# Two unused tiles that shift the weight buffers by 32 bytes, in a two-layer hybrid decoder trunk

## The chip, the core and the metric

The kernel runs on one core of a Trainium2 chip, in one launch. The time is the device time of that core in microseconds (us). Five engines work side by side and meet through semaphores: TensorE (PE, with its weight loads shown apart as PEld), VectorE (DVE), ScalarE (ACT), GpSimd (POOL) and SyncE (SP, which issues most DMAs here). Lower is better.

A matmul has two operands in on-chip memory (SBUF). The stationary one, 128 columns of fp32, is put into the array by an LDWEIGHTS instruction; the moving one, up to 512 columns, is then streamed through by the MATMUL. The LDWEIGHTS of the next matmul runs while the present one streams, so that two reads of SBUF by TensorE go on at the same time, at addresses that the allocation of tiles decides.

## The reference

Two layers, each a pair of token mixers in parallel and then a gated feed-forward network, on 1024 tokens of 1024 features, all in fp32. Cut to what matters:

```python
for l in range(DEPTH):                                   # DEPTH = 2
    h = rmsnorm(x, norm1[l])
    proj = h @ w_in[l]                                   # 1024 x 5120: q, k, v of two mixers, and gates
    qa, ka, va, qb, kb, vb, gate_pre = jnp.split(proj, splits, axis=-1)
    o_a = dilated_mixture(hd4(qa, DSW_HEADS), hd4(ka, DSW_HEADS), hd4(va, DSW_HEADS))
    o_b = stick_breaking_attention(hd4(qb, SB_HEADS), hd4(kb, SB_HEADS), hd4(vb, SB_HEADS))
    g_a, g_b = split(jax.nn.sigmoid(gate_pre + b_gate[l]))
    merged = g_a * (o_a @ w_br[l, :OUT_A]) + g_b * (o_b @ w_br[l, OUT_A:])
    x = x + merged @ w_o[l]                              # 1024 x 1024
    h2 = rmsnorm(x, norm2[l])
    a, v = split(h2 @ w_up[l])                           # 1024 x 5632
    a = causal_depthwise_conv(a, conv_w[l], conv_b[l])
    x = x + (jax.nn.gelu(a, approximate=False) * v) @ w_down[l]   # 2816 x 1024
return rmsnorm(x, norm_f)
```

## The kernel before

**Arithmetic.** Each fp32 operand of a product is held in two parts of type fp32r, a rounded high part and the rest (`split`: ACT writes the high part, L145, DVE the low one, L153). A product is then three matmuls, high by high, high by low and low by high. In `seven` (L1055, its matmuls L1058 to L1060) and `product_of` (L1818 to L1820) these three stand next to each other. The large projections are done in blocks with seven products for eight (`seven` is one such product). Nearly all matmuls have 128 rows, 128 stationary columns and 512 moving columns.

**Where the operands lie.** A weight block arrives by DMA as raw fp32, and `piece` (L1049) or `weights` splits it into two tiles of 128 x 512, with the tags `wh` (high, named `w_hi`) and `wl` (low, `w_lo`), four buffers each. These eight buffers of 2048 bytes per partition are what the change moves. They serve as the stationary operand in the input projection (outputs `i_a`, `i_b`, `i_c`), the up projection (`u_a`, `u_b`, `u_c`, and `u_ps` for its first columns), the output projection (`o_ps`), and in about half of the down projection (`d_ps`; the other half has its parts in tiles `wd` of the tag `p4`). Only in two short places are they the moving operand: `v_ps<-w_hi,hh` at the very start (192 matmuls of 256 columns) and `f_ps` at the very end (36 of 512). The moving operands are activations: `hh` and `hl` (the normed input in two parts), `t_hi` and `t_lo` (sums of blocks of it) and `gd_in` (the gated values, back from DRAM).

**The order.** TensorE's order is written out by hand; ACT, DVE and POOL are scheduled, in part in written order too. In each layer there is a first stretch in which the input projection is interleaved with the attention work (transposes `sb_t` and `v_t`, scores `z`, values `sb_o`), then the output projection, the up projection and the down projection. The pool `sb` gives every tag its place in SBUF in the order in which tags are first asked for, each rounded up to 32 bytes. The tags `wh` and `wl` are first asked for in `first()`, by the first call of `weights_hi`.

Of the kernel before, what the change touches and what calls it, by code (L numbers as in the profile page):

```python
# [7 lines left out]
F32 = mybir.dt.float32  # L8
# [8 lines left out]
P = 128  # L17
# [48 lines left out]
def trunk_kernel(ctx, tc, x, norm1, vecs, w_in, w_br, w_o, w_up, w_down, norm_f, out, depth=None, probe=None):  # L66
# [6 lines left out]
    sb = ctx.enter_context(tc.tile_pool(name="sb", bufs=1))  # L73
# [300 lines left out]
    def attend(dense, items):  # L374

        late = None
        for i, (name, first, rest, rate, make) in enumerate(items):
            if i == 0:  # L380
                dense.until(first)
                dense.step()
                dense.step()
                sc, micro = make()
                for f in sc:
                    f()
                    dense.advance(rate)
                dense.done.add(name + "s")
# [269 lines left out]
    def values_on(o, todo, part_, first, last):  # L658

        todo = sorted(todo, key=lambda x: x[1].start - x[1].stop)  # L660
        for i, (vals, to, at) in enumerate(todo):
            pe.matmul(o[:, to], vals, part_[0][:, at], start=(first and i == 0), stop=False, skip_group_check=True)
        for i, (vals, to, at) in reversed(list(enumerate(todo))):
            pe.matmul(o[0:LOW, to], vals[:, 0:LOW], part_[1][:, at], start=False, stop=(last and i == 0), skip_group_check=True)
# [1345 lines left out]
    def first():  # L2010
# [17 lines left out]
        def weights_hi(r):  # L2028
            hi = sb.tile([P, 2, 256], F32R, tag="wh", bufs=4, name="w_hi")
            lo = sb.tile([P, 2, 256], F32R, tag="wl", bufs=4, name="w_lo")  # L2030
            act.copy(hi, raw[:, r : r + 2, :])
            wv.extend((hi[:, i, :], lo[:, i, :]) for i in range(2))
            parts[r] = hi, lo
# [13 lines left out]
        def scaled(i):  # L2047
            if i in (0, 2):
                rest["pair"] = big("xsq")
            sq = rest[i] = rest["pair"][:, i % 2, :] if i < 4 else sb.tile([P, T], F32, tag="ot", name="xsq")  # L2050
            ss = factor[i] = sb.tile([P, 8], F32, tag="ss", bufs=2, name="ss")
            with tc.high_priority(offset=AHEAD):
                one = act.activation(sq, xr[i], AF.Square, accum_out=ss[:, 0:1])
                if i >= TWICE + 2:
                    tc.add_manual_dep(one.ins, LAST["kept" if i == 5 else f"hi{max(2, i - 3)}"], NO_SYNC, reason="behind")
                act.activation(ss[:, 1:2], ss[:, 0:1], AF.Sqrt, bias=eps[:, 0:1], scale=1.0 / D)
                one = dve.reciprocal(ss[:, 2:3], ss[:, 1:2])
            if i == 0:
                tc.add_manual_dep(one.ins, LAST["base"], NO_SYNC, reason="in turn")
            yield  # L2060
            if i < TWICE:
                for h in range(2):
                    hd = slice(h * HF, (h + 1) * HF)
                    dve.scalar_tensor_tensor(sq[:, hd], xr[i][:, hd], ss[:, 2:3], gb[h], ALU.mult, ALU.mult)
            yield
# [48 lines left out]
        def fill(n):  # L2114

            for _ in range(n):
                pe.matmul(wp[:, 0:P], ident, ident, start=True, stop=True)
# [15 lines left out]
            pe.transpose(gb[k // 4][:, (k % 4) * P : (k % 4 + 1) * P], g0[:, k : k + 1].to_broadcast([P, P]), ident)  # L2133
        f = [scaled(i) for i in range(8)]
        next(f[0])
        weights_hi(0)
        weights_hi(2)
        fill(4)
        next(f[0])
# [90 lines left out]
```

## Time and profile before

| | |
|---|---|
| median of 3 runs | 2599.28 us (2599.11 to 2599.80) |
| profiled execution | 2600.39 us |
| its span, first to last instruction | 2598.4 us |
| PE busy in the span | 2585.0 us (99%), 12600 matmuls |
| PEld / DVE / ACT / POOL busy | 2161.4 / 2088.0 / 1340.1 / 105.5 us |
| mean granted TensorE clock | 0.999 |
| bytes moved by DMA | 470.59 MB, 181 GB/s in the mean |

A row of the groups' view gives line, engine, operation, output and inputs, shape and count, then busy time and mean duration. The duration of a MATMUL reaches from its start to its modelled end and overlaps with the next ones (some 389 ns for 512 columns); what a matmul costs in a dense stretch is the distance from its start to the next start, and that is read from the timeline, whose first column is the start in us. A row of the timeline with x4 stands for four instructions in a row.

### The profile page before, as it was taken

The page shows a single profiled execution, that of the slowest core. Times are in us where ns is not written, and L with a number is a line of the kernel's source. Part 1 is how long each engine was busy: PE and PEld are TensorE (multiplying, and loading weights), DVE is VectorE, ACT ScalarE, POOL GpSimd, SP SyncE. Part 2 cuts the span into 40 slices and gives each one's busy share as a digit, 9 for nine tenths or more (in the row PEclk, how much of TensorE's full clock was granted, in tenths as well). Part 3 has the DMA queues.
Part 4 walks back from the last instruction along what each step waited for, and adds up shares of the span by engine and source line. Part 5 has one row for each costly group of instructions (what it writes and reads, how often), then busy time and mean ns, then how long its engine had stood idle before and what let it go on. Part 6 is the DMA issues. An engine that isn't in the chain of part 4 may idle for free.

```text
span 2598.4 us, 35940 instructions
## 1 busy us (share of the span) xinstructions
PE 2585.0 (99%) x12600; PEld 2161.4 (83%) x12600; DVE 2088.0 (80%) x3482; ACT 1340.1 (52%) x2506; POOL 105.5 (4%) x145
## 2 busy tenths in 40 slices
PE   9999999999999999999999999999999999999999
PEld 8888888888888888888888888888888888888887
DVE  8878777795988888897678788777869888889966
ACT  6555666573554555422445565666645555544223
POOL 3000000030000000000000000000300000000000
PEclk9999999999999999999999999999999999999999
DMA  7534588973344444688444446798633344456963
GB/s 256 153 119 134 161 209 225 236 237 97 90 146 157 143 163 146 235 327 315 152 143 148 126 132 175 199 238 239 205 99 121 125 154 154 140 176 246 346 242 134
DMA packets 400772, 470.59 MB, mean 181 GB/s; under 512 B 24616, under 2 KB 315856, under 8 KB 398800
## 3 DMA queue, kind: packets, MB, share of 16 engines
q1 hardware_dynamic: 399728, 465.90, 56.1%
q0 software_dynamic: 704, 2.13, 0.4%
q8 instruction: 100, 1.64, 0.3%
q14 instruction: 80, 0.66, 0.1%
q10 hardware_dynamic: 160, 0.27, 0.0%
HBM read 305.59 MB, written 162.63 MB: 180 GB/s over the span
## 4 chain that ended last, share of the span: by engine, by line
PE 92%; DVE 4%; ACT 2%; DMA 1%; issue 1%; POOL 0%; DVEq 0%; ACTq 0%; POOLq 0%
PE u_a L1058 5%; PE u_a L1059 5%; PE u_a L1060 5%; PE d_ps L1818 5%; PE d_ps L1819 5%; PE d_ps L1820 5%; PE i_a L1058 5%; PE i_a L1059 5%; PE i_a L1060 5%; PE u_c L1058 3%; PE u_c L1059 3%; PE u_c L1060 3%; PE i_c L1058 2%; PE i_c L1060 2%; PE i_c L1059 2%; PE o_ps L188 2%
## 5 line engine op out<-in xcount | busy, mean ns | idle before, releaser
L145 ACT CAST w_hi<-up_a 128x512 fp32r<-128x512 f32 x280 | 173.9, 622 | 277.2 <-DVE up_a L1672 120.8
L153 DVE TENSOR_TENSOR w_lo<-up_a,w_hi 128x512 fp32r<-128x512 f32 x280 | 189.5, 689 | 83.5 <-ACT w_hi L145 83.5
L145 ACT CAST w_hi<-in_a 128x512 fp32r<-128x512 f32 x252 | 156.3, 622 | 161.6 <-PE i_c L1059 33.2
L153 DVE TENSOR_TENSOR w_lo<-in_a,w_hi 128x512 fp32r<-128x512 f32 x252 | 172.8, 688 | 72.6 <-ACT w_hi L145 60.6
L1829 DVE TENSOR_TENSOR x<-x,d_ps 128x512 f32<-128x512 f32 x220 | 150.2, 684 | 60.5 <-PE d_ps L1820 57.2
L1058 PE MATMUL u_a<-hh,w_hi 128*128 128x512 f32 x320 | 124.5, 389 | 0.0
L1060 PE MATMUL u_a<-hh,w_lo 128*128 128x512 f32 x320 | 124.5, 389 | 0.0
L1059 PE MATMUL u_a<-t_lo,w_hi 128*128 128x512 f32 x320 | 124.5, 389 | 0.0
L1060 PE MATMUL u_a<-t_hi,w_lo 128*128 128x512 f32 x320 | 124.5, 389 | 0.0
L1059 PE MATMUL u_a<-hl,w_hi 128*128 128x512 f32 x320 | 124.5, 389 | 0.0
L1058 PE MATMUL u_a<-t_hi,w_hi 128*128 128x512 f32 x320 | 124.5, 389 | 0.0
L1818 PE MATMUL d_ps<-gd_in,w_hi 128*128 128x512 f32 x316 | 123.2, 390 | 0.0
L1819 PE MATMUL d_ps<-gd_in,w_hi 128*128 128x512 f32 x316 | 123.0, 389 | 0.0
L1820 PE MATMUL d_ps<-gd_in,w_lo 128*128 128x512 f32 x316 | 123.0, 389 | 0.0
L1058 PE MATMUL i_a<-hh,w_hi 128*128 128x512 f32 x288 | 117.8, 409 | 0.0
L1058 PE MATMUL i_a<-t_hi,w_hi 128*128 128x512 f32 x288 | 116.5, 404 | 0.0
L1060 PE MATMUL i_a<-hh,w_lo 128*128 128x512 f32 x288 | 113.1, 393 | 0.0
L1060 PE MATMUL i_a<-t_hi,w_lo 128*128 128x512 f32 x288 | 113.0, 392 | 0.0
L1059 PE MATMUL i_a<-t_lo,w_hi 128*128 128x512 f32 x288 | 113.0, 392 | 0.0
L1059 PE MATMUL i_a<-hl,w_hi 128*128 128x512 f32 x288 | 112.9, 392 | 0.0
L1818 PE MATMUL d_ps<-gd_in,wd 128*128 128x512 f32 x284 | 110.9, 390 | 0.0
L1820 PE MATMUL d_ps<-gd_in,wd 128*128 128x512 f32 x284 | 110.5, 389 | 0.0
(403 smaller groups left out, 7723.4 us busy)
## 6 DMA issues: line engine op xcount, KB each, us to landing
gd<-g SPq DMA_DIRECT2D x154, 512.0 KB, 3.1
gd_in<-gd SPq DMA_DIRECT2D x154, 512.0 KB, 6.0
up_a<-in_w_up_dram SPq DMA_DIRECT2D x80, 512.0 KB, 5.4
in_a<-in_w_in_dram SPq DMA_DIRECT2D x72, 512.0 KB, 5.4
wd_raw<-in_w_down_dram SPq DMA_DIRECT2D x22, 1024.0 KB, 10.9
gin<-gs SPq DMA_DIRECT2D x32, 512.0 KB, 4.5
w_raw<-in_w_o_dram SPq DMA_DIRECT2D x64, 256.0 KB, 3.0
gs<-u SPq DMA_DIRECT2D x48, 256.0 KB, 3.2
```

Source lines behind the costliest of these rows:

```text
L145: one = act.copy(hi, src)
L153: two = dve.tensor_tensor(lo, src, f32(hi), ALU.subtract)
L188: pe.matmul(o, lh, rl, start=False, stop=False, skip_group_check=share)
L1058: pe.matmul(o, w[0][:, c], rh, start=(first and i == 0), stop=False, skip_group_check=True)
L1059: pe.matmul(o, w[0][:, c], rl, start=False, stop=False, skip_group_check=True)
L1060: pe.matmul(o, w[1][:, c], rh, start=False, stop=(last and i == 3), skip_group_check=True)
L1818: pe.matmul(o, wh[:, c], gh, start=(i == 0 and k in (0, 4, 5)), stop=False, skip_group_check=True)
L1819: pe.matmul(o, wh[:, c], gl, start=False, stop=False, skip_group_check=True)
L1820: pe.matmul(o, wl[:, c], gh, start=False, stop=(i == m - 1), skip_group_check=True)
L1829: dve.tensor_tensor(x, x, o, ALU.add)
```

## The change

In `first()`, a tile of 8 fp32 (32 bytes per partition) is asked for just ahead of the first `weights_hi`, and one of 24 fp32 (96 bytes) just behind it. Nothing writes or reads them. Since a tag gets its place when it is first asked for, the eight buffers of `wh` and `wl` stand between the two.

```diff
         f = [scaled(i) for i in range(8)]
         next(f[0])
+        sb.tile([P, 8], F32, tag="below", name="below")
         weights_hi(0)
+        sb.tile([P, 24], F32, tag="above", name="above")
         weights_hi(2)
```

`weights_hi`, which asks for the two tags, is

```python
        def weights_hi(r):
            hi = sb.tile([P, 2, 256], F32R, tag="wh", bufs=4, name="w_hi")
            lo = sb.tile([P, 2, 256], F32R, tag="wl", bufs=4, name="w_lo")
            act.copy(hi, raw[:, r : r + 2, :])
```

Start addresses in each partition, as the two programs are built:

| buffers | before | changed | before, over a multiple of 256 | changed |
|---|---|---|---|---|
| `t_hi`, `t_lo`, some `gd_in` (first of six) | 8480 | 8480 | 32 | 32 |
| `wd`, `beta` (first of four) | 57632 | 57632 | 32 | 32 |
| `w_hi` (first of four) | 86304 | 86336 | 32 | 64 |
| `w_lo` (first of four) | 94496 | 94528 | 32 | 64 |
| `hh` of the first half, some `gd_in` | 102688 | 102816 | 32 | 160 |
| `kv`, `slots` (first of four) | 151840 | 151968 | 32 | 160 |
| `hh` of the second half | 192800 | 192928 | 32 | 160 |

Before, all operands of the fp32r matmuls begin 32 bytes over a multiple of 256, and so do all the slices of them that matmuls use, since these are cut at whole 128 columns (512 bytes). After the change the weight parts alone begin at a multiple of 64 (64 over a multiple of 128), and all others still begin 32 over a multiple of 128. The instructions of each engine, and the order in which they stand, are the same in both programs.

## The prediction

> **What bounds the kernel now.** I read the page first, its busy times, its slices and its chain of waits.
>
> ```profile
> span 2598.4 us, 35940 instructions
> PE 2585.0 (99%) x12600; PEld 2161.4 (83%) x12600; DVE 2088.0 (80%) x3482; ACT 1340.1 (52%) x2506; POOL 105.5 (4%) x145
> PEclk9999999999999999999999999999999999999999
> PE 92%; DVE 4%; ACT 2%; DMA 1%; issue 1%; POOL 0%; DVEq 0%; ACTq 0%; POOLq 0%
> ```
>
> PE is busy in 99% of the span at a clock that stays at its top digit, and 92% of the chain that ended last lies on it. The view of waits, for PE alone, says how much of the rest the other engines hold:
>
> ```profile
> PE warm L2117 <- POOL ident masks.py:199: 1.8, 1, 1.8
> PE v_ps L189 <- DVE hl L153: 1.0, 2, 0.8
> PE o_ps L188 <- POOL hl L1436: 0.7, 1, 0.7
> ```
>
> The longest wait of PE on another engine is 1.8 us in all. So the time is the sum of the distances between the starts of matmuls, and a change of operand addresses can act only through them. The timeline of PE in the up projection, first and last row of 61 matmuls:
>
> ```profile
> 900.13 0.39 PE L1058 MATMUL u_a<-hh,w_hi 128*128 128x512 f32 x1
> ...
> 913.73 0.39 PE L1058 MATMUL u_a<-t_hi,w_hi 128*128 128x512 f32 x1
> ```
>
> 60 distances in 13.60 us are 226.67 ns each. The second reading is where the value projection of the second layer begins, with 256 moving columns (19 distances from the second row to the last):
>
> ```profile
> 1304.10 0.28 PE L187 MATMUL v_ps<-v_w,hh 128*128 128x256 f32 x1
> 1304.21 0.28 PE L188 MATMUL v_ps<-v_w,hh 128*128 128x256 f32 x1
> ...
> 1306.49 0.28 PE L189 MATMUL v_ps<-v_w,hl 128*128 128x256 f32 x1
> ```
>
> 2.28 us / 19 are 120.0 ns. Two points give a line: (226.67 - 120.0) / 256 = 0.4167 ns per moving column, and 226.67 - 512 x 0.4167 = 13.3 ns per matmul that do not depend on the columns streamed. The first distance here, 0.11 us, is shorter than the later 0.12: the fixed part is not simply paid at each start. These 13.3 ns are what is in question. They could be a fixed price of changing the stationary operand, or reads of the next weights that get in the way of the stream; only the second could hang on addresses.
>
> **The change part by part.** It removes and adds no instruction, moves none, and changes no wait, so nothing has a duration of its own. What changes is where eight buffers stand. How many matmuls does that touch? The counts, from the views of lines 1058 and 1059 and from the groups (durations there are minimum/median/maximum in ns; each row stands for one of the three lines of its product, and the other two have as many):
>
> ```profile
> L1058 PE MATMUL u_a<-hh,w_hi x320: 389/389/390, 711.2 to 2376.7; 128*128 128x512 f32 x160
> L1058 PE MATMUL i_a<-hh,w_hi x288: 387/395/481, 65.0 to 1817.7; 128*128 128x512 f32 x144
> L1059 PE MATMUL i_a<-hl,w_hi x288: 387/393/398, 65.2 to 1817.9; 128*128 128x512 f32 x144
> L1058 PE MATMUL u_c<-t_hi,w_hi x160: 389/389/390, 714.0 to 2363.1; 128*128 128x512 f32 x160
> L1058 PE MATMUL u_b<-hh,w_hi x160: 388/389/390, 725.4 to 2374.0; 128*128 128x512 f32 x160
> L1058 PE MATMUL i_c<-t_hi,w_hi x144: 387/394/481, 67.7 to 1798.4; 128*128 128x512 f32 x144
> L1058 PE MATMUL i_b<-hh,w_hi 128*128 128x512 f32 x144 | 59.2, 411 | 0.0
> L1818 PE MATMUL d_ps<-gd_in,w_hi 128*128 128x512 f32 x316 | 123.2, 390 | 0.0
> L187 PE MATMUL o_ps<-hh,w_hi 128*128 128x512 f32 x256 | 100.1, 391 | 0.2 <-DVE x L1327 0.2
> L187 PE MATMUL u_ps<-hh,w_hi 128*128 128x512 f32 x128 | 50.2, 392 | 0.0
> ```
>
> `u_a` and `u_c` come with both kinds of moving operand, `hh` and `t_hi`, so that they count six times: 6 x 320 + 6 x 160 + 3 x 160 = 3360 for the up projection; in the same way 6 x 288 + 6 x 144 + 3 x 144 = 3024 for the input projection; 3 x (316 + 256 + 128) = 2100 for the other three. That makes 8484 matmuls whose weights begin 32 bytes elsewhere relative to what streams beside them. One nanosecond on each would be 8.5 us, 0.33% of the time.
>
> *First term, the spacing of those 8484.* The trace has no fp32r matmul with the new distance, so it is bounded from both sides. The lower bound is the whole 13.3 ns gone: -113 us. The upper one is the worst that the same matmuls show today. That is found in the input projection:
>
> ```profile
> 302.64 0.48 PE L1058 MATMUL i_b<-hh,w_hi 128*128 128x512 f32 x1
> 302.95 0.40 PE L1059 MATMUL i_b<-hl,w_hi 128*128 128x512 f32 x1
> ...
> 304.11 0.60 PE L1294 MATMUL v_t<-ident,u 128*128 128x128 f32 x4
> 304.47 0.48 PE L1058 MATMUL i_b<-hh,w_hi 128*128 128x512 f32 x1
> 304.78 0.39 PE L1059 MATMUL i_b<-hl,w_hi 128*128 128x512 f32 x1
> ...
> 305.94 0.40 PE L662 MATMUL sb_o<-sbh,kv 128*128 128x256 f32 x2
> ...
> 306.64 0.39 PE L1059 MATMUL i_a<-hl,w_hi 128*128 128x512 f32 x1
> ...
> 307.55 0.39 PE L1060 MATMUL i_a<-hh,w_lo 128*128 128x512 f32 x1
> ```
>
> Behind a group of transposes, five matmuls take 1.16 us, 232 ns each, twice over; the four distances from 306.64 to 307.55 take 0.91 us and are back at 227. All relative addresses are the same, so the distance hangs on timing, by 5.3 ns here over the 226.67. If all 5460 matmuls that run at 226.67 now (8484 less the 3024) went to 232, that would be +29 us.
>
> Between -113 and +29 I take 0, for three reasons in the trace. First, the stream walks 512 columns, 2048 bytes, while the weights walk 512 bytes: at different speeds the two pass each other through every distance within a single matmul, so another start only moves the moment at which they meet. Second, the fixed part does not follow how much is read. In the attention some loads have 66 columns in place of 128:
>
> ```profile
> L662 PE MATMUL sb_o<-sbh,kv 128*128 128x256 f32 x128 | 28.2, 281 | 0.4 <-DVE vv L1300 0.4
> L664 PE MATMUL sb_o<-sbl,kv 128*66 128x256 f32 x128 | 28.2, 281 | 0.0
> ```
>
> Half the weights and the same 281 ns; stolen slots would have come down by half of 13.3. Third, in the up projection the minimum, median and maximum are 389/389/390 ns over 320 matmuls that use four different buffers of weights and four slices of each, against moving operands in several places: what the addresses differ in now (multiples of 256 bytes, by the addresses ahead of this section) leaves no trace at all.
>
> A rule of the Trainium skill bears on this (TensorE: Matmul & The Clock Gate, "Part 2: What happens when you issue a matmul"): it gives TensorE two independent read ports into SBUF, so that loading the next weights takes no bandwidth from the running stream. By it the term is 0. The page's spacing of warm matmuls (its section "Back-to-back issue gap"), N / 2.4 + 2.5 ns, makes 215.8 ns for 512, and the trace does not agree: 226.67. If the 10.8 ns between were a conflict that the shift undoes, an estimate from that page would be 8484 x 10.8 = -92 us.
>
> *Second term, the writers.* ACT and DVE now write the parts at the new address, from sources at the old one. The nearest rows are those of the norm, in which two of the 32 have a source that begins at a multiple of 64 beside another operand 32 off:
>
> ```profile
> L558 DVE TENSOR_TENSOR hl<-b_f,hh x32: 679/684/693, 640.3 to 1970.2; 128x512 fp32r<-128x512 f32 x32
> ```
>
> All lie within 693 / 684 = 1.3% above the median and 0.7% below. DVE and ACT carry 4 + 2% of the chain, 156 us; 1.3% of that is +2.0 us, 0.7% is -1.1. I take 0: the matmuls ahead of a part are the cover, and PE's waits above show that the cover holds. Without it, some 9 ns would be paid for each part that is made.
>
> *Sum.* 2600.4 us for the profiled execution (2598.4 of span and 2.0 around it), plus 0 and 0. The median of the runs stands 1.1 us below that execution, and I carry this over: 2599.3 us.
>
> **The rivals.**
>
> *The load and the stream collide now, and 32 bytes part them.* For it speaks that 13.3 ns per matmul are paid and that the distance varies with timing, which a mere fixed price would not. Against it, the three reasons. In full it would give 2599.3 - 113 = 2486 us; half of it 2543. Chance 0.07.
>
> *The input projection settles.* Its irregular distances are the one place where timing between load and stream is seen. If another phase let `i_a` and its like fall to the 389 ns of the up projection from the medians of 393 to 395 in the rows, 4 ns (most have the 393) on 3024 matmuls are 12 us: 2587 us. Against it: the irregularity follows transposes, whose operands lie outside the moved buffers. Chance 0.04.
>
> *The up and down projections lose their step.* The regular 226.67 ns may be a locked state of load and stream, which the equal addresses bring about. Shifted, they would run as the input projection does behind transposes: +29 us, 2628 us. It decides (over 0.2%, 5.2 us) from about 980 matmuls on that lose 5.3 ns. For it: both spacings exist with the same instruction. Against it: `i_a` comes back to the short spacing by itself (306.64 to 307.55), so that the state restores itself when it is disturbed. Chance 0.11.
>
> *The change does not do what it says.* If the pool gave the tiles another place, no address would move; the addresses ahead show that it does not, and the time would be the forecast's.
>
> **How the numbers follow.** No effect: 0.78, which has 2599.3 with some 2 us on either side (the second term). Faster: 0.07 + 0.04 = 0.11. Slower: 0.11. A difference under 0.2% is not told from none here, so these are also the chances by that bound. For the range I reach from 2599.3 towards the two near rivals: down to 2590, which takes in three quarters of a settling input projection, and up to 2606, which takes in a lost step in a fifth of the matmuls. With the 0.78 that holds a little over 0.8; the full forms of the first and third rival stay outside.
>
> **What would show it.** In the changed trace, 60 distances of `u_a` and `u_c` matmuls in 13.60 us again, 19 of `v_ps` in 2.28, `i_a` at 387/395/481, and PE busy at 2585 us: then the addresses do nothing. A spacing near 213 would show the first rival, and `i_a` at 389/389/390 the second. Rows of `u_a` with a spread like that of `i_a` would show the third. The forecast is wrong if any of the 8484 distances moves by 0.6 ns in the mean. If they don't and the time does, the writers or a DMA are the place to look.

## The result, and the profile after

The changed kernel takes 2646.76 us (median of 4 runs, 2645.30 to 2647.36) against 2599.27 us (4 runs, 2599.11 to 2599.80): 1.0182 of the time before, with a 95% interval of 1.0169 to 1.0194. That is 47.5 us slower, where 2599.3 (2590 to 2606) was forecast.

The head of the page of the changed kernel, its chain of waits by engine, and the longest entries of PE's own waits:

```profile
span 2643.5 us, 35940 instructions
PE 2632.9 (100%) x12600; PEld 2162.0 (82%) x12600; DVE 2089.7 (79%) x3482; ACT 1340.1 (51%) x2506; POOL 104.9 (4%) x145
PEclk9999999999999999999999999999999999999999
PE 96%; DVE 2%; ACT 1%; DMA 0%; issue 0%; POOL 0%; DVEq 0%; ACTq 0%; POOLq 0%
PE warm L2117 <- POOL ident masks.py:199: 1.8, 1, 1.8
PE v_ps L189 <- DVE hl L153: 0.9, 2, 0.7
```

The span grew by 45.1 us and PE's busy time by 47.9, while the other engines and the weight loads (PEld, 2161.4 before) stayed within 2 us. The clock did not drop (its digits are 9 throughout), and PE waits for others as little as before. So the whole loss lies in the distances between the starts of matmuls. Two stretches of the up projection in the timeline of the changed kernel, each by its first and last row:

```profile
914.22 0.39 PE L1058 MATMUL u_a<-hh,w_hi 128*128 128x512 f32 x1
...
915.62 0.40 PE L1058 MATMUL u_c<-t_hi,w_hi 128*128 128x512 f32 x1
...
921.22 0.40 PE L1058 MATMUL u_c<-hh,w_hi 128*128 128x512 f32 x1
...
929.63 0.39 PE L1058 MATMUL u_a<-hh,w_hi 128*128 128x512 f32 x1
```

From 914.22 to 929.63 there are 66 distances: 233.5 ns each, in place of 226.67. The 24 from 915.62 to 921.22, all with `t_hi` or `t_lo` as the moving operand, take 5.60 us, 233.3 ns. In the view by tile (minimum/median/maximum of the durations in ns) the same shows without counting:

```profile
L1058 PE MATMUL u_a<-hh,w_hi x320: 392/392/392, 716.7 to 2416.3; 128*128 128x512 f32 x160
L1060 PE MATMUL u_a<-hh,w_lo x320: 399/399/399, 717.1 to 2416.7; 128*128 128x512 f32 x160
L1058 PE MATMUL u_a<-t_hi,w_hi x320: 388/395/398, 722.3 to 2410.7; 128*128 128x512 f32 x160
L1058 PE MATMUL i_a<-hh,w_hi x288: 388/394/484, 64.5 to 1843.0; 128*128 128x512 f32 x144
L1819 PE MATMUL d_ps<-gd_in,wd x284: 387/398/404, 1148.4 to 2621.5; 128*128 128x512 f32 x142
L187 PE MATMUL br_ps<-oh_a,br_w x64: 389/389/389, 540.0 to 1885.2; 128*128 128x512 f32 x64
L1058 PEld LDWEIGHTS u_a<-hh,w_hi x320: 187/188/188, 716.4 to 2416.0; 128*128 128x128 f32 x160
```

The same rows of the kernel before, for `d_ps` and `br_ps`:

```profile
L1819 PE MATMUL d_ps<-gd_in,wd x284: 387/389/396, 1131.1 to 2576.5; 128*128 128x512 f32 x142
L187 PE MATMUL br_ps<-oh_a,br_w x64: 389/389/390, 537.2 to 1859.8; 128*128 128x512 f32 x64
```

The 389 of `u_a` has become a pattern that repeats with the three lines of a product. `br_ps`, neither of whose operands moved relative to the other, still has 389. `d_ps<-gd_in,wd` has lost its 389 too, although `wd` did not move: its moving operand did, by 128 bytes. The weight load itself is as long as it was.

All distances of the two traces, from one start to the next, summed by output (the 5460 are those that the prediction counted as regular):

| matmuls | count | before, us | change, us | mean before, after, ns |
|---|---|---|---|---|
| up projection `u_a`, `u_b`, `u_c` | 3360 | 762.7 | +22.15 | 227.0, 233.6 |
| the 5460: the row above, `d_ps` with `w_hi`/`w_lo` (+6.0), `o_ps` (+3.3), `u_ps` (+2.3) | 5460 | 1242.0 | +33.8 | 227.5, 233.7 |
| input projection `i_a`, `i_b`, `i_c` | 3024 | 712.5 | +7.4 | 235.6, 238.1 |
| weights not moved, moving operand moved: `d_ps` with `wd` (+5.0), the query and key products `q_ps`, `kq_ps` (+1.0) | 1044 | 237.8 | +6.1 | 227.8, 233.6 |
| `br_ps`, neither moved | 384 | 87.0 | +0.05 | 226.7, 226.8 |
| all other | | | -2.3 | |

Without the first row, which is part of the second, they add up to the growth of the span, 45.05 us before rounding.

### The profile page after: what moved, and what is told of

The parts are those of the page before. It is cut to its first block, busy times and chain, and to the rows that moved or that the text cites. A ratio compares the mean times of both kernels' runs of the same rounds, so it can differ in the third digit from the quotient of the medians.

```text
span 2643.5 us, 35940 instructions
## 1 busy us (share of the span) xinstructions
PE 2632.9 (100%) x12600; PEld 2162.0 (82%) x12600; DVE 2089.7 (79%) x3482; ACT 1340.1 (51%) x2506; POOL 104.9 (4%) x145
## 4 chain that ended last, share of the span: by engine, by line
PE 96%; DVE 2%; ACT 1%; DMA 0%; issue 0%; POOL 0%; DVEq 0%; ACTq 0%; POOLq 0%
PE u_a L1060 6%; PE u_a L1059 6%; PE u_a L1058 6%; PE d_ps L1819 5%; PE d_ps L1818 5%; PE d_ps L1820 5%; PE i_a L1058 5%; PE i_a L1059 5%; PE i_a L1060 5%; PE u_c L1060 3%; PE u_c L1058 3%; PE u_c L1059 3%; PE i_c L1059 2%; PE i_c L1058 2%; PE i_c L1060 2%; PE o_ps L187 2%
```

## The experiments

Four theories stood against each other. **A**: the spacing hangs on the distance between the stationary and the moving operand, modulo 256 bytes; zero is special. **B**: it hangs on where the weights begin, at a multiple of 64 now. **C**: any move of the buffers does it. **D**, asked later: some distance is better than zero.

**The spacing by itself, `m1_scan`.** A kernel that leaves the whole computation of the reference out and runs blocks of 48 matmuls (`hi` by `hi`, `hi` by `lo`, `lo` by `hi`) between one region of weights and one of moving data, with a shift of one, of the other, or of both. Block names give the shift in steps of 32 bytes (`fine_` in steps of 4).

```diff
+    def block(name, dw, dm, n=512, cols=P, turns=4):
+        for i in range(4 * turns):
+            c = i % 4
+            hi, lo = (wt[:, a + dw + P * c : a + dw + P * c + cols] for a in (0, 2048))
+            hh, hl = (mv[:, a + dm + 512 * c : a + dm + 512 * c + n] for a in (0, 4096))
+            pe.matmul(o[0:cols, 0:n], hi, hh, ...)
+            pe.matmul(o[0:cols, 0:n], hi, hl, ...)
+            pe.matmul(o[0:cols, 0:n], lo, hh, ...)
```

> A kernel that leaves the whole computation out and runs only blocks of 48 matmuls (36 or 84 in a few) of the form of the projections: stationary 128 columns, moving 512, high by high, high by low, low by high, with the weights moved by a step of 32 bytes per block relative to the moving operand (blocks by_zero to by_sixteen), the same behind four transposes (disturbed_), by steps of 4 bytes (fine_), with the moving operand moved in place of the weights (moving_), both together (both_), with 256 moving columns (half_) and with 64 stationary columns (narrow_). Theory A (the distance between weights and moving operand decides, in a period of 256 bytes): by_zero, by_eight and by_sixteen at 226.7 ns, that is a mean duration of 389 ns, the blocks between at 231 to 238 ns (393 to 400), the moving_ blocks a mirror of the by_ blocks, all both_ blocks at 226.7. Rival B (where the weights begin by themselves, a multiple of 64 being bad): by_one, by_three and so on at 233 and by_zero, by_two and so on at 226.7, both_ like by_, moving_ all at 226.7. Rival C (not the address but the surroundings in the full kernel): every block with 512 columns at 226.7 ns.

Its timeline, 30 distances late in three blocks, first and last row of each:

```profile
49.68 0.39 PE L92 MATMUL by_zero<-mv,wt 128*128 128x512 f32 x1
...
56.48 0.39 PE L92 MATMUL by_zero<-mv,wt 128*128 128x512 f32 x1
...
60.64 0.40 PE L92 MATMUL by_one<-mv,wt 128*128 128x512 f32 x1
...
67.64 0.40 PE L92 MATMUL by_one<-mv,wt 128*128 128x512 f32 x1
...
115.91 0.39 PE L92 MATMUL by_six<-mv,wt 128*128 128x512 f32 x1
...
122.78 0.39 PE L92 MATMUL by_six<-mv,wt 128*128 128x512 f32 x1
```

These are 226.7 ns at distance 0, 233.3 at 32 bytes and 229.0 at 192. The steady spacing of all blocks, from their starts (the last 35 distances of each, in the one execution that was run):

| shift in bytes | 0 | 32 | 64 | 96 | 128 | 160 | 192 | 224 | 256 |
|---|---|---|---|---|---|---|---|---|---|
| of the weights | 226.66 | 233.37 | 233.40 | 234.29 | 232.37 | 233.37 | 228.80 | 233.29 | 226.69 |
| of the moving operand | | 233.31 | 228.83 | 233.4 | 233.46 | 234.29 | 233.4 | 233.37 | 226.66 |

From 288 to 512 the weights' row repeats, and the moving operand's row is the weights' row read backwards but for 128. Shifting both by the same amount leaves 226.66 to 226.69 at all eight shifts. The view by tile shows the mirror and the joint shift:

```profile
L92 PE MATMUL by_six<-mv,wt x16: 388/388/397, 113.8 to 124.1; 128*128 128x512 f32 x16
L92 PE MATMUL moving_two<-mv,wt x16: 388/388/398, 532.7 to 543.0; 128*128 128x512 f32 x16
L92 PE MATMUL both_four<-mv,wt x16: 389/389/398, 654.3 to 664.5; 128*128 128x512 f32 x16
```

So the distance decides and its period is 256 bytes, in a kernel that holds nothing but these matmuls. Theory A had expected 231 to 238 ns at all distances but 0; the 228.8 at 192 bytes lies below that. In the changed kernel the distance is 32 bytes beside `t_hi` and `t_lo`, 160 beside `hh` and `hl` (64 - 160, modulo 256), and 128 where `wd` meets a moved `gd_in`. The scan has 233.4, 233.4 and 232.4 to 233.5 ns there, and the table above 233.6 for the up projection and the 1044.

"In step" is used from here on for the short regular spacing. How distance 0 comes to its short spacing is seen behind four transposes:

```profile
235.98 0.60 PE L100 MATMUL turned<-ident,wt 128*128 128x128 f32 x4
236.34 0.48 PE L92 MATMUL disturbed_zero<-mv,wt 128*128 128x512 f32 x1
236.66 0.39 PE L93 MATMUL disturbed_zero<-mv,wt 128*128 128x512 f32 x1
...
238.04 0.39 PE L93 MATMUL disturbed_zero<-mv,wt 128*128 128x512 f32 x1
...
239.40 0.39 PE L93 MATMUL disturbed_zero<-mv,wt 128*128 128x512 f32 x1
```

Behind a first distance of 320 ns, the six from 236.66 to 238.04 take 231 ns each in the mean (1.385 us in the unrounded trace; single ones 227 to 236) and the six behind them 226.7: about seven matmuls are spent on getting into step. In the second scan, further down, it took up to ten. In the input projection the prediction quoted the same: distances of 232 behind transposes, of 227 later. Blocks of 256 columns run at 120.0 ns at distance 0 and 256 and at 117.3 to 120.0 at the others; blocks with 64 stationary columns run at 229.9 at 0 and between 228.3 (at 192 bytes) and 232.7 (at 64). The good distance holds for this shape only. The changed kernel agrees: `v_ps`, with 256 moving columns, has left distance 0 and takes 0.6 us less.

**All buffers by 32, `e1_all32`.** The first tile stands before every other buffer, so that all operands move together. It is asked for at the start of `first()`.

```diff
+        sb.tile([P, 8], F32, tag="below", name="below")
```

> One tile of 32 bytes ahead of everything in the pool, so that weights and moving operands all begin at 64 over a multiple of 256 and keep their distances; as the change, the weights begin at a multiple of 64. Theory A (distance): 2599 us, within 0.2%. Rival B (where the weights begin): about 2645 us. Rival C (any move of the buffers): about 2645 us.

2597.96 us (10 runs, 2597.16 to 2600.69) against 2599.39, ratio 0.9996 (0.9986 to 1.0005). By tile:

```profile
L1058 PE MATMUL u_a<-hh,w_hi x320: 389/389/389, 709.3 to 2374.2; 128*128 128x512 f32 x160
L1059 PE MATMUL i_a<-hl,w_hi x288: 387/393/398, 65.1 to 1815.9; 128*128 128x512 f32 x144
```

The kernel before has 389/389/390 and 387/393/398 in these rows. The weights begin at a multiple of 64 here as in the changed kernel, every buffer has moved, and nothing is lost. B and C fall.

**Weights by 256, `e2_weights256`.** The same place as in the change, with a period's length and nothing above.

```diff
+        sb.tile([P, 64], F32, tag="below", name="below")
         weights_hi(0)
```

> 256 bytes below the weight buffers and nothing above, so that they and all above them move by 256 bytes. Theory A with a period of 256 bytes or a part of it: 2599 us. Theory A with a longer period, or rival C (any move): 2630 to 2650 us. Rival B (where the weights begin, by 64): 2599 us.

2599.27 us, ratio 0.9999 (0.9990 to 1.0009). The buffers have other addresses and the time is the same: the period of 256 holds in the kernel too.

**Upper buffers by 128, `e3_upper128`.** The weight parts stay; what lies above them, `hh` among it, moves by 128, and `t_hi` stays.

```diff
         weights_hi(0)
+        sb.tile([P, 32], F32, tag="above", name="above")
```

> Nothing below the weight buffers and 128 bytes above them: the weights stay, and hh, hl, part of gd_in, kv and slots move by 128 bytes, as they do in the change. Theory A with a period of 256: matmuls with these moving operands rise to some 233 ns (1920 of 3360 in the up projection, all of the output projection, most of the down projection, half of the input projection), which makes about +30 us, 2630 us; those with t_hi stay at 226.7. Theory A with a period of 128 or less, or rival B (where the weights begin): 2599 us, except that the wd matmuls of the changed kernel (+5 us there) need another cause.

2631.94 us, ratio 1.0123 (1.0107 to 1.0139). Three rows of its groups (busy us, mean ns):

```profile
L1058 PE MATMUL u_a<-hh,w_hi 128*128 128x512 f32 x320 | 126.4, 395 | 0.0
L1058 PE MATMUL u_a<-t_hi,w_hi 128*128 128x512 f32 x320 | 124.6, 389 | 0.0
L1819 PE MATMUL d_ps<-gd_in,wd 128*128 128x512 f32 x284 | 112.0, 394 | 0.0
```

The same weights in the same projection run at 389 with `t_hi` (distance 0) and at 395 with `hh` (distance 128). The weight parts did not move, and yet the span grew by 31.3 us: 12.8 of them in the up projection, 6.7 ns on each of its 1920 matmuls with `hh` or `hl`, 5.5 in `d_ps` with `wd`, the rest in the other products with a moved operand.

**Weights by 32 and nothing else, `e4_rel32`.** The padding above makes up 256, so that only the eight weight buffers change their distance.

```diff
+        sb.tile([P, 8], F32, tag="below", name="below")
         weights_hi(0)
+        sb.tile([P, 56], F32, tag="above", name="above")
```

> 32 bytes below the weight buffers and 224 above, so that the weights stand 32 bytes off all moving operands, and all moving operands keep their distances among themselves and to the other stationary ones (wd, kq_w) over a period of 256. The words of the change, without the 128 bytes by which it also moves hh, hl and gd_in. Theory A (distance over a period of 256): the first scan gives 233.4 ns at 32 bytes; the 5460 regular matmuls with such weights rise by 6.7 ns (36.6 us), those of the input projection, 3 ns less, by 8 us in all; wd, kq_w and q_ps stay. About 2643 us, between 2635 and 2645. If the 128 bytes were the whole cause (rival), 2599 us.

2639.80 us, ratio 1.0159 (1.0144 to 1.0174). In its groups the up projection has lost its step and `wd` has nearly kept it:

```profile
L1058 PE MATMUL u_a<-hh,w_hi 128*128 128x512 f32 x320 | 126.6, 396 | 0.0
L1819 PE MATMUL d_ps<-gd_in,wd 128*128 128x512 f32 x284 | 110.7, 390 | 0.0
```

The up projection is longer by 21.6 us, 6.4 ns each, where the scan has 6.7; the input projection by 7.2; `q_ps`, `kq_ps` and `br_ps` by nothing. `d_ps` with `wd` still loses 1.2 us, although its distance is 0. Its matmuls alternate with those of the parts and have to find their step anew behind them: 1.1 of the 1.2 us fall on the first nine matmuls of each run of `wd` (230.7 ns in the mean, 228.4 before), and the later ones have 226.9 (226.7 before).

**Weights by 192, `e5_rel192`.** The one distance among the multiples of 32 that the scan puts near zero's spacing.

```diff
+        sb.tile([P, 48], F32, tag="below", name="below")
         weights_hi(0)
+        sb.tile([P, 16], F32, tag="above", name="above")
```

> 192 bytes below the weight buffers and 64 above: the weights stand 192 bytes off all moving operands. The first scan has 228.8 ns there, 2.1 ns over the best, and reaches it at once behind a disturbance, where the distance 0 needs six matmuls at some 231. Theory A (the scan's distances hold in the full kernel): +2.1 ns on 5460 matmuls is +11.7 us, and about -1 ns on 3024 of the input projection -3 us, so about 2608 us. Rival (any distance but 0 loses the regular state and costs the same): about 2640 us.

2610.50 us, ratio 1.0045 (1.0028 to 1.0062).

```profile
L1058 PE MATMUL u_a<-hh,w_hi x320: 388/394/394, 711.2 to 2385.4; 128*128 128x512 f32 x160
L1059 PE MATMUL u_a<-hl,w_hi x320: 388/388/392, 711.4 to 2385.6; 128*128 128x512 f32 x160
```

The up projection is longer by 7.3 us over 3360 matmuls, 2.2 ns each; the scan has 228.80 - 226.66 = 2.1. The input projection, which was expected to gain 3 us, lost 0.8. For the regular stretches the spacings of the scan carry over to the kernel, and a multiple of 64 is no better or worse than its distance makes it.

**Every multiple of 4 bytes, `m2_scan`.** Again without the computation of the reference; each block stands behind four transposes. It adds blocks in which only one part of an operand is shifted.

```diff
+        for k in range(64):
+            disturb()
+            block(f"fine_{WORDS[k // 8]}_{WORDS[k % 8]}", k, 0)
+        ...    # mix_: hi by one shift, lo by another; low_: the low moving operand alone
```

> A kernel that leaves the whole computation out: blocks of 48 matmuls behind four transposes, with the weights moved by 0 to 252 bytes in steps of 4 (fine_, the name counts eighths: fine_two_three is 19 x 4 bytes), with the high weights moved by a and the low ones by b steps of 32 bytes (mix_), and with the low moving operand moved by steps of 32 (low_). Theory A: 226.7 ns in the steady state at fine_zero_zero, mix_zero_zero and low_zero; 228 to 235 ns elsewhere; mix_ with one of the two at 0 between. Rival D (226.7 is no floor but one point of a curve): some distance lies below 226.7 ns, towards the 213 that the moving columns alone would take. Whether a distance exists that is as good in the steady state and better behind a disturbance is open.

Of 64 distances, six have a steady spacing of 226.66 to 226.69: 0, 16, 28, 120, 132 and 240 bytes. The others lie between 229 and 243, and none is below. D falls. Theory A had expected only zero at 226.7 and nothing above 235. Where the high and the low part have different shifts, the spacing is 228.8 to 235.5, and with the low moving operand alone shifted 229.0 to 233.4. At 16 bytes the matmuls behind the transposes are in step at once (behind the first distance, six of 226.7 in the mean, where distance 0 has 232.5):

```profile
L92 PE MATMUL fine_zero_four<-mv,wt x16: 389/389/475, 93.4 to 103.7; 128*128 128x512 f32 x16
```

In the first scan the same 16 bytes, entered from another block and not from transposes, had run at 233.4:

```profile
L92 PE MATMUL fine_four<-mv,wt x16: 394/394/394, 465.9 to 476.4; 128*128 128x512 f32 x16
```

**Would 16 or 28 bytes make the kernel faster? `e6_parts0`, `e7_parts16`, `e8_parts28`.** The pool rounds each buffer to 32 bytes, so the eight weight buffers are cut by hand out of one tile, at an offset of 0, 16 and 28 bytes (`SHIFT` of 0, 4 and 7). They are handed out in a fixed round: a part can be overwritten while it is still needed and some waits differ, so the computation is changed, and the control with offset 0 is what the other two are compared with.

```diff
+SHIFT = 0
...
+            PARTS.append(sb.tile([P, 8 * 512 + 8], F32R, tag="parts", name="parts"))
+            sb.tile([P, 56], F32, tag="above", name="above")
...
+        return (PARTS[0][:, SHIFT + at : SHIFT + at + 512] ... for at in (512 * i, 2048 + 512 * i))
...
-                hi = sb.tile([P, per, cols], F32R, tag="wh", bufs=4, name="w_hi")
-                lo = sb.tile([P, per, cols], F32R, tag="wl", bufs=4, name="w_lo")
+                hi, lo = w_parts(cols)
```

> The eight weight buffers cut by hand from one tile, at the same addresses as before the change; the control for the next two. Every theory: within 0.2% of 2599 us.

> The same one tile with all weight parts 16 bytes further. In the second scan the distance 16 has 226.7 ns at once behind a disturbance, where 0 needs six matmuls at some 231; in the first scan, entered from another block, it had 233.4. Theory A with a best state that is entered at once: the regular stretches keep 226.7, the input projection comes down from 229.8 (without the matmuls behind transposes) to about 227, some 8 us, so 2591 us. Rival (two steady states at this distance, and the entry decides): part of the stretches at 233.4, up to 2640 us.

> The same with 28 bytes, the other distance at which the second scan has 226.7 ns at once. Theory A with a best state that is entered at once: about 2591 us. Rival (two steady states, the entry decides): up to 2640 us.

2618.61 us for the control (ratio 1.0076, 1.0060 to 1.0091, to the kernel before), 2651.42 at 16 bytes (1.0201, 1.0187 to 1.0215) and 2656.53 at 28 (1.0207, 1.0187 to 1.0226). The control missed its expectation of 0.2%: 17.4 us went into the distances of `u_ps`, in which PE now waits 12.3 us for parts. Against the control, 16 bytes are 32.8 us slower and 28 bytes 37.9, so neither offset gains anything. At 28 bytes one of five executions took 2641.41 us and the others 2653.71 to 2656.87; what differed in it was not recorded. By tile, the first row from the control and the second from 16 bytes:

```profile
L1068 PE MATMUL u_a<-hh,parts 128*128 128x512 f32 x320 | 124.5, 389 | 0.0
```

```profile
L1068 PE MATMUL u_a<-hh,parts x320: 394/396/398, 724.4 to 2426.8; 128*128 128x512 f32 x160
L1828 PE MATMUL d_ps<-gd_in,parts x316: 389/389/468, 1116.4 to 2628.9; 128*128 128x512 f32 x158
```

The same 16 bytes are slow in the whole up projection and mostly fast in the down projection. The timeline of the down projection shows where it changes (`wd` lies at distance 0 here):

```profile
1151.74 0.39 PE L1828 MATMUL d_ps<-gd_in,parts 128*128 128x512 f32 x1
...
1156.17 0.39 PE L1829 MATMUL d_ps<-gd_in,parts 128*128 128x512 f32 x1
...
1156.63 0.39 PE L1828 MATMUL d_ps<-gd_in,wd 128*128 128x512 f32 x1
...
1158.01 0.39 PE L1828 MATMUL d_ps<-gd_in,wd 128*128 128x512 f32 x1
...
1202.21 0.39 PE L1828 MATMUL d_ps<-gd_in,parts 128*128 128x512 f32 x1
...
1206.97 0.39 PE L1828 MATMUL d_ps<-gd_in,parts 128*128 128x512 f32 x1
```

Up to 1156.17 the parts run at 233.2 ns (19 distances in 4.43 us). Then matmuls with `wd` at distance 0 take six distances of 231 in the mean and fall into step, and when parts at 16 bytes come again they stay in it: 21 distances from 1202.21 to 1206.97 take 4.76 us, 226.7 ns each. At 16 bytes there are two steady states and the entry decides; distance 0 is the one at which the short spacing restored itself wherever it was watched.

No version was found that beats the kernel before. By the scan it already has the best of the eight distances that its pool can give.

## Why the prediction was wrong

**What bounds the kernel** was read rightly: no wait, no clock and no other engine moved, and the loss is the sum of start-to-start distances. **The second term** (the writers) was right at 0. The low part's writer by tile, of the kernel before and of the changed one:

```profile
L153 DVE TENSOR_TENSOR w_lo<-up_a,w_hi x280: 679/690/695, 708.6 to 2367.9; 128x512 fp32r<-128x512 f32 x140
```

```profile
L153 DVE TENSOR_TENSOR w_lo<-up_a,w_hi x280: 680/690/695, 713.7 to 2407.1; 128x512 fp32r<-128x512 f32 x140
```

690 ns both times.

**The first term failed**: the spacing of the 8484, put at nothing. Of its bounds, -113 to +29, 0 was taken, and the measured value is +41.2 on the 8484 matmuls (33.8 on the 5460 regular ones, 7.4 in the input projection), outside the upper bound. Each of the three reasons for 0 fell:

- *The stream passes through every distance anyway, so the start does not matter.* The scan shows that the start decides: 226.66 at 0 and 233.37 at 32 bytes, in a steady state over dozens of matmuls. The spacing behaves like a state that a distance keeps up, and that restores itself at distance 0 in seven to ten matmuls. That load and stream hold one another in it is a reading; no run shows the reads themselves.
- *The fixed part does not follow how much is read* (66 columns and 128, 281 ns both). The row was true, of the distances too (118.4 and 118.3 ns), and the inference was not. Those were matmuls of 256 columns, for which zero is not the good distance (120.0 at 0, 117.3 at 96 bytes). With 64 stationary columns and 512 moving ones, distance 0 is not the good one either (229.9, and 228.3 at 192 bytes). The 13.3 ns were drawn as a line through two points that both had distance 0; since the same instructions have other spacings at other distances, they are no fixed price of a matmul.
- *What the addresses differ in now leaves no trace* (389/389/390 over many buffers). They differed in multiples of 256 bytes, which is the period. The row could not speak on a shift of 32, however many buffers it covered. This reason weighed most and carried nothing.

The Trainium skill (TensorE: Matmul & The Clock Gate, "Part 2: What happens when you issue a matmul") says that the two reads have ports of their own and that a load takes no bandwidth from the running stream. By that the distance would not matter, and these runs do not agree: the same instructions are 6.7 ns apart by the distance of their operands alone.

**The rivals.** *The up and down projections lose their step* was what happened: equal addresses (modulo 256) bring about the short spacing, and the shift takes it away. The sign that it named, `u_a` rows with a spread like that of `i_a`, came only in part: with `t_hi` there is a spread (388 to 398), but with `hh` each line has one duration (392 and 399 in the rows shown). The matmuls did not go over to the irregular spacing behind transposes but to other regular ones. So its price was mis-sized. It took 5.3 ns from matmuls that were on their way back into step; a lasting wrong distance costs 6.6 in the up projection (22.15 us / 3360), and over the 5460 it came to 33.8 and not 29. It left the input projection out, where the stretches between disturbances had been in step: +7.4. And the count of touched matmuls, 8484, was too small: the table of addresses showed that `hh` and some `gd_in` move by 128 while `wd` and the other weights stay, so another 1044 with 512 columns change their distance, for +6.1. Nor do all of the 8484 stand 32 bytes off: beside `hh` the distance became 160. The chance of 0.11 rested on "the state restores itself when it is disturbed", which is true of distance 0, the one that was about to be given up; behind transposes the scan's blocks at 32 bytes come back to 233.3 in the same way. The observation was evidence for the lock and was counted against it. *A collision now* would have gone to 2486: no distance of the 64 has a steady spacing below 226.66. *The input projection settles*: it went the other way.

**What stays open**: what the hardware does in the 13 ns; why the period is 256 bytes; whether the pair that counts is the two operands of one matmul, or the stream of one and the weights of the next, which are loaded beside it (the scans shift both alike); and whether a shift of 16 bytes with buffers handed out as before could hold 226.7 ns every time; that was not tried.

## What to carry to other kernels

For matmuls that each load new weights of 128 columns beside 512 moving ones of fp32r, give the stationary and the moving operands start addresses that are equal modulo 256 bytes, and look again after any new tile: two unused tiles of 32 and 96 bytes cost 1.8% here, and one of 128 bytes 1.2%. With 256 moving columns the scan had no gain from distance 0. A row with no spread says that something is in step, not that it can't be put out of it; ask what all its instances have in common before it is used as evidence. Of a shift of buffers, count the pairs of operands whose distance changes, not the buffers that were meant to move.

## What was not expected of the hardware

The distance between the two operands of a matmul, modulo 256 bytes, sets its spacing: 226.7 ns at 0, 228.8 at 192, 232.4 to 234.3 at the other multiples of 32, up to 243 at multiples of 4, five of which (16, 28, 120, 132 and 240 bytes) also reach 226.7 behind transposes. At 16 bytes two steady states, 226.7 and 233.4, exist for the same instructions, and 21 distances of the down projection held the first after matmuls at distance 0 had set it. After four transposes, distance 0 needs seven to ten matmuls to come into step; in the first scan six of them run at 231 ns in the mean.
